# A hybrid-branch layer on one core: order of the Fourier weight products, pooling products one block earlier, the output gate multiplied into the output weights

## The chip, the cores and the metric

The program runs on one core of a Trainium2 chip. Its engines have separate instruction streams: PE (TensorE, matrix products into PSUM accumulators), DVE (VectorE) and ACT (ScalarE) for elementwise work, POOL (GpSimd), and SP (SyncE), which here only issues DMA transfers. The metric is the device time of one execution in microseconds (us), lower is better; times are medians of several runs.

## The reference, cut to what matters

One layer over 1024 latent tokens and 256 context tokens of width 1024, in float32:

```python
h = rms_norm(x + sincos) * (1 + scale) + shift            # modulated by c @ ada_w
u_lru, z_lru, u_fft, z_fft, u_pool, z_pool, gates = split(h @ w_in)
y_lru  = scan(forward) + scan(backward)                   # per-channel linear recurrences
y_fft  = einsum(real(fft2(u_fft by groups)), fft_w)       # 4 groups of 128 channels
y_pool = einsum(windowed means - u_pool, pool_w) * pool_scale   # 4 groups of 128 channels
m = sum over the branches of sigmoid(gate_b) * ((y_b * silu(z_b)) @ proj_b)
x = x + gt[None, :] * (m @ w_out)                         # gt: 1024 values, from c @ ada_w
out = rms_norm(x, final_g)
```

## The kernel before, in words

**Products.** Every large float32 product runs on TensorE as three products of a high and a low part (`mm3`, L190: low weights times high data, high times low, high times high). So each operand is first cut in two by `split` (L125): ACT copies the high part (L129), DVE subtracts to get the low part (L134). Data lies with channels on partitions, in tiles of 128 x 1024 tokens; an accumulator is one of four PSUM tiles of 128 x 1024 (`acc`), which comes free when its last reader is done.

**Middle part.** TensorE's instructions stand in the program in the order of a list of units (L1111 to L1120), worked off by one loop. A unit `("g4", 0)` is the first half of the 48 products of one 128-column block of the input projection; `m0` to `m3` are the pooling branch's products (6 each, `MP`, L1002), `c0` to `c7` that branch's output projection (24 products each, over all four pooling groups), `s`, `t` and `b` the same for the Fourier branch, `pa` for the recurrent branch. Loads and vector steps are hooked to places of this list by `on(place, function)`. Order on the other engines, SP's DMA queue among them, is set by a scheduler that simulates the program; what it chose is fixed when the kernel is built. Blocks that are not needed at once are parked in DRAM (`keep`, L84) and loaded again (`fetch`, L106).

`group_dft` (L910) computes two plain (not split) products with a 512-wide operand into the two halves of one accumulator `pq`, and splits each. `load_pool(n)` (L992) fetches one pooling tile `pp` and splits it into `ph` and `pl`; it is hooked three units ahead of `m`n, and `load_z("p", n)` two ahead. `MP` multiplies its result with `zp` on DVE and splits it again into `c`n`h` and `c`n`l`.

**Last part.** The output weights `wo` come in eight tiles; `split_wo` (L1069) splits each raw tile. `gate_rows` spreads the gate `gt` over the partitions (`gt["b"]`, a 128 x 1024 tile, called `gtb` at the end). In the last stage all engines follow the written order: for each of eight row tiles of 128 tokens there are 48 products with `wo`, then `finish` (L1236) multiplies the sums with `gtb`, adds the residual, squares with a running sum on ACT, takes the root and its reciprocal, and scales with the final gain `fgt`. The last row tile (`finish_last`, L1257) is cut in columns 0 to 511, 512 to 767 and 768 to 1023 (`CUTS`, L1255) so that its vector work follows its products closely; its first cut is multiplied with `fgt` on POOL and scaled on ACT.

Of the kernel before, what the change touches and what calls it, by code (L numbers as in the profile page):

```python
# [9 lines left out]
AF = mybir.ActivationFunctionType  # L10
ALU = mybir.AluOpType

D = 1024
# [3 lines left out]
HALF = 512  # L17
EPS = 1e-6
# [10 lines left out]
def tile_hybrid_mixer(  # L29
# [26 lines left out]
    V, S, G, PE, SP = nc.vector, nc.scalar, nc.gpsimd, nc.tensor, nc.sync  # L56
# [11 lines left out]
    def f4(name, shape=(128, 1024), pool=None):  # L68
        return (pool or p4).tile(list(shape), F32, tag="t4", name=name)

    def f2(name, shape=(128, 512)):
        return p2.tile(list(shape), F32, tag="t2", name=name)
# [4 lines left out]
    def r2(name, shape=(128, 512)):  # L77
        return p2.tile(list(shape), F32R, tag="t2", name=name)

    def acc(name):  # L80
        return pacc.tile([128, 1024], F32, tag="acc", name=name)
# [31 lines left out]
    def act(o, i, func=AF.Identity, **kw):  # L113
        S.activation(out=o, in_=i, func=func, **kw)  # L114

    def tt(o, a, b, op):
        V.tensor_tensor(o, a, b, op=op)  # L117

    def stt(o, a, s, b, op0, op1, **kw):
        V.scalar_tensor_tensor(o, a, s, b, op0=op0, op1=op1, **kw)  # L120
# [6 lines left out]
    def split(hi, lo, src, eng="act", low="dve"):  # L127
        if eng == "act":
            S.copy(hi, src)  # L129
        elif eng == "pool":  # L130
            G.tensor_scalar(hi, src, 1.0, 0.0, op0=ALU.mult, op1=ALU.add)
        else:
            V.tensor_copy(hi, src)
        (G if low == "pool" else V).tensor_tensor(lo, src, f(hi), op=ALU.subtract)  # L134
# [55 lines left out]
    def mm3(o, pairs, first=True, last=True):  # L190
        n = len(pairs)
        for i, (wh, wl, xh, xl) in enumerate(pairs):
            PE.matmul(out=o, lhsT=wl, rhs=xh, start=first and i == 0, stop=False)  # L193
            PE.matmul(out=o, lhsT=wh, rhs=xl, start=False, stop=False)  # L194
            PE.matmul(out=o, lhsT=wh, rhs=xh, start=False, stop=last and i == n - 1)  # L195
# [6 lines left out]
    eps = const.tile([128, 1], F32, name="eps")  # L202
    sc = const.tile([128, 160], F32, name="sc")
    b1 = sc[:, 0:8]
# [5 lines left out]
    c4 = sc[:, 64:80]  # L210
# [31 lines left out]
    with tc.manual_schedule(engines={ET.PE}):  # L242
# [132 lines left out]
        t0, t1, t2, t3 = tmp  # L375
# [534 lines left out]
        def group_dft():  # L910
            cg, fw = pq["cg"], pq["fw"]
            pq["h"], pq["l"] = [], []
            ps = acc("pq")
            for n in range(2):
                PE.matmul(out=ps[:, H[n]], lhsT=cg[:, n * 128:(n + 1) * 128], rhs=fw, start=True, stop=True)
                hi, lo = r2(f"pqh{n}"), r2(f"pql{n}")
                split(hi, lo, ps[:, H[n]])
                pq["h"].append(hi)
                pq["l"].append(lo)
# [144 lines left out]
        wof = {}  # L1064
# [2 lines left out]
            wof[k] = Weight(f"wo{k}", wo[k], (128, 1024), (praw,) + ((pwt, pwt) if k < 3 else (p4, p4)))  # L1067

        def split_wo(k):  # L1069
            w = wof.pop(k).ready()  # L1070
            woh[k], wol[k] = w.hi, w.lo

        diag, gt = {}, {}
# [33 lines left out]
        def halves(*keys):  # L1107
            return [(k, h) for k in keys for h in range(2)]
# [4 lines left out]
        units = halves("ZP0", "ZP1", "ZP2", "ZP3")  # L1113
        LRU_AT = {}
        for j in range(NK):
            LRU_AT[j] = len(units)
            units += halves(f"u{j}", *others[4 * j:4 * j + 4])
        units += halves("g4", "g5") + ["m0"] + halves("g6") + ["m1", "m2"] + halves("g7")
        units += ("m3 c0 c1 s0 c2 s1 t0 c3 s2 t1 c4 s3 t2 c5 t3 c6 c7 b0 b1 b2 b3 b4 b5 b6 b7").split()
        units += halves(*[f"pa{n}" for n in range(NK)])  # L1120
        pos_of = {u: n for n, u in enumerate(units)}
        wkeys = []
# [12 lines left out]
        def on(u, func, *a, table=ev):  # L1135
            u = pos_of[u] if not isinstance(u, int) else u
            table.setdefault(u, []).append(lambda: func(*a))
# [15 lines left out]
            for k, n in AT:  # L1153
                on(LRU_AT[j] + n, pieces[k], table=ev if k == "w" else aft)

        on(pos_of["g4", 0] - 1, load_poolw)
        on(pos_of["g4", 0], load_dft)
        on(pos_of["g5", 0], group_dft)
        for n in range(4):
            on(pos_of[f"m{n}"] - 3, load_pool, n)  # L1160
# [17 lines left out]
        for k in range(3):  # L1178
            on(A0 + 10 + k, load_wo, k)
            on(A0 + 12 + k, split_wo, k)  # L1180
# [15 lines left out]
        late = 0  # L1196
        flush_stores(len(units))
        assert not ev and not aft, (ev.keys(), aft.keys())
        gtb = gt.pop("b")
        for k in range(NK):  # L1200
            yh[k] = yl[k] = None

# [1 line left out]
        for k in range(3, NK):  # L1204
            load_wo(k)
            split_wo(k)
        strict.enter_context(tc.manual_schedule(engines=REST))
        fgt = f4("fgt")
# [27 lines left out]
        def finish(i):  # L1236
            o = po.pop(i)
            r = xp.pop(i)
            q = f4(f"q{i}")
            ss = rss[:, 2 * (i % 8):2 * (i % 8) + 2]  # L1240
            for h in range(2):
                sl = slice(h * HALF, (h + 1) * HALF)
                tt(q[:, sl], o[:, sl], gtb[:, sl], ALU.mult)
                tt(r[:, sl], r[:, sl], q[:, sl], ALU.add)
                act(q[:, sl], r[:, sl], AF.Square, accum_out=ss[:, h:h + 1])
            tt(ss[:, 0:1], ss[:, 0:1], ss[:, 1:2], ALU.add)
            act(ss[:, 0:1], ss[:, 0:1], AF.Sqrt, scale=1.0 / D, bias=eps)
            V.reciprocal(ss[:, 0:1], ss[:, 0:1])
            for h in range(2):
                sl = slice(h * HALF, (h + 1) * HALF)  # L1250
                stt(q[:, sl], r[:, sl], ss[:, 0:1], fgt[:, sl], ALU.mult, ALU.mult)
                SP.dma_start(out=out[i * 128:(i + 1) * 128, sl], in_=q[:, sl])


        CUTS = ((0, 512), (512, 768), (768, 1024))  # L1255

        def finish_last(i):  # L1257
            r = xp.pop(i)
            ss = rss[:, 0:4]
            parts = []  # L1260
            for n, (lo, hi) in enumerate(CUTS):
                o = acc(f"o{i}_{n}")
                mm3(o[:, 0:hi - lo], [(mh[k][:, i * 128:(i + 1) * 128], ml[k][:, i * 128:(i + 1) * 128],
                                       woh[k][:, lo:hi], wol[k][:, lo:hi]) for k in range(NK)])
                if n == 0:
                    finish(i - 1)
                p, q = f2(f"rp{n}"), f4(f"rq{n}", (128, 512))
                p, q = p[:, 0:hi - lo], q[:, 0:hi - lo]
                parts.append((p, q))
                tt(q, o[:, 0:hi - lo], gtb[:, lo:hi], ALU.mult)  # L1270
                tt(p, r[:, lo:hi], q, ALU.add)
                act(q, p, AF.Square, accum_out=ss[:, n:n + 1])
            tt(ss[:, 0:1], ss[:, 0:1], ss[:, 1:2], ALU.add)
            tt(ss[:, 0:1], ss[:, 0:1], ss[:, 2:3], ALU.add)
            act(ss[:, 0:1], ss[:, 0:1], AF.Sqrt, scale=1.0 / D, bias=eps)
            G.tensor_tensor(parts[0][0], parts[0][0], fgt[:, 0:HALF], op=ALU.mult)
            V.reciprocal(ss[:, 0:1], ss[:, 0:1])  # L1277
            for (lo, hi), (p, q) in zip(CUTS, parts):
                if lo:
                    stt(q, p, ss[:, 0:1], fgt[:, lo:hi], ALU.mult, ALU.mult)  # L1280
                else:
                    act(q, p, scale=ss[:, 0:1])
                SP.dma_start(out=out[i * 128:(i + 1) * 128, lo:hi], in_=q)


        for k in range(NK):
# [2 lines left out]
        for i in range(7):  # L1289
            if 2 < i + 3 < 8:  # L1290
                load_res(i + 3)
            if 2 < i < 6:
                WO(i + 1, range(NK), True, True)
            finish(i) if i < 6 else None
        finish_last(7)
        strict.close()

# [91 lines left out]
```

## Time and profile before

| what | value |
|---|---|
| runs | 1024.05, 1025.68, 1026.28 us; median 1025.68 |
| profiled execution | 1026.29 us, of which 1024.3 us are the span of the trace |
| TensorE busy | 993.5 us (97%) |
| VectorE busy | 604.0 us (59%) |
| ScalarE busy | 537.7 us (52%) |
| GpSimd busy | 25.1 us (2%) |
| moved by DMA | 152.59 MB, 149 GB/s on average |

The span runs from the first to the last event of the trace; the profiled execution's own time has some 2 us around it. Busy shares are means over all stages; what one stage costs is read from the rows of its own stretch. Matrix products overlap: a row's duration is longer than the step to the next row.

### The profile page before, as it was taken

Reading aid. Unit: us, or ns where it says so; the run is one execution under the profiler, and the core shown is the slowest. Engines: PE = TensorE matmul, PEld = TensorE weight load, DVE = VectorE, ACT = ScalarE, POOL = GpSimd, SP = SyncE. Lnnn points to the kernel's source line nnn. Section 1 sums busy time; section 2 is a strip of 40 time slices with the busy share of each in tenths; the row PEclk is TensorE's granted clock in tenths of the full one; section 3 lists DMA queues with packets and bytes.
Section 4 is the critical chain, followed back from the end, with each engine's and each line's share of the span. In section 5 each row is a group of like instructions: output and inputs, shape, how many; then the busy total and the mean of one; then the engine's idle time right before and its main releaser. Section 6 shows DMA issues by size and latency. Waiting matters only on the chain. (4 is left out here: it accounts for less than half of the span.)

```text
span 1024.3 us, 11615 instructions
## 1 busy us (share of the span) xinstructions
PE 993.5 (97%) x4572; PEld 821.0 (80%) x4572; DVE 604.0 (59%) x770; ACT 537.7 (52%) x632; POOL 25.1 (2%) x23
## 2 busy tenths in 40 slices
PE   7999999999999999999999999979899999999995
PEld 5867888888888888888888888858698888888885
DVE  6969286448485575936638274345465763444177
ACT  4543553793957859688694966914232221222122
POOL 0000000000000000000000000000000000000232
PEclk9999999999999999999999999989899999999998
DMA  9541694133322323343423322437445793325053
GB/s 347 196 154 42 208 411 167 66 103 132 104 83 72 124 93 124 123 154 103 154 103 116 105 78 72 148 135 272 139 170 208 265 325 129 124 103 165 19 198 121
DMA packets 47656, 152.59 MB, mean 149 GB/s; under 512 B 5489, under 2 KB 8177, under 8 KB 47602
## 3 DMA queue, kind: packets, MB, share of 16 engines
q1 hardware_dynamic: 47602, 151.85, 41.7%
q8 instruction: 36, 0.59, 0.2%
q14 instruction: 18, 0.15, 0.0%
HBM read 114.08 MB, written 37.75 MB: 148 GB/s over the span
## 5 line engine op out<-in xcount | busy, mean ns | idle before, releaser
L114 ACT ACT_TABLE_LOAD x71 | 91.1, 1283 | 1.9 <-PEq L1379 0.7
L120 DVE SCALAR_TENSOR_TENSOR junk<-ada,sb 128x1024 bf16<-128x1024 f32 x32 | 39.0, 1219 | 23.6 <-DMA ada<-in_ada 22.9
L193 PE MATMUL pg<-hh,g_l 128*128 128x512 f32 x128 | 51.3, 401 | 0.0
L194 PE MATMUL o<-wo_l,mh 128*128 128x512 f32 (+1 forms) x136 | 51.2, 377 | 0.0
L195 PE MATMUL o<-wo_h,mh 128*128 128x512 f32 (+1 forms) x136 | 51.2, 376 | 0.0
L193 PE MATMUL o<-wo_h,ml 128*128 128x512 f32 (+1 forms) x136 | 51.2, 376 | 0.0
L194 PE MATMUL pg<-hl,g_h 128*128 128x512 f32 x128 | 50.5, 395 | 0.0
L195 PE MATMUL pg<-hh,g_h 128*128 128x512 f32 x128 | 50.5, 394 | 0.0
L193 PE MATMUL ppa<-yh,pa_l 128*128 128x512 f32 x128 | 50.2, 392 | 0.0
L193 PE MATMUL ph<-hh,h_l 128*128 128x512 f32 x128 | 49.9, 389 | 0.0
L195 PE MATMUL ppa<-yh,pa_h 128*128 128x512 f32 x128 | 49.8, 389 | 0.0
L195 PE MATMUL ph<-hh,h_h 128*128 128x512 f32 x128 | 49.8, 389 | 0.0
L194 PE MATMUL ph<-hl,h_h 128*128 128x512 f32 x128 | 49.8, 389 | 0.0
L194 PE MATMUL ppa<-yl,pa_h 128*128 128x512 f32 x128 | 49.8, 389 | 0.0
L193 PE MATMUL pu<-hh,u_l 128*128 128x512 f32 x128 | 49.8, 389 | 0.0
L194 PE MATMUL pu<-hl,u_h 128*128 128x512 f32 x128 | 49.8, 389 | 0.0
L195 PE MATMUL pu<-hh,u_h 128*128 128x512 f32 x128 | 49.8, 389 | 0.0
L193 PE MATMUL pi<-hh,i_l 128*128 128x512 f32 x128 | 49.8, 389 | 0.0
L194 PE MATMUL pi<-hl,i_h 128*128 128x512 f32 x128 | 49.8, 389 | 0.0
L195 PE MATMUL pi<-hh,i_h 128*128 128x512 f32 x128 | 49.8, 389 | 0.0
L114 ACT ACTIVATE gc<-bdc,sml 64x256 f32<-64x256 f32 x64 | 30.1, 470 | 33.1 <-PE bdc L694 32.2
L117 DVE TENSOR_TENSOR i<-i,xc 128x1024 f32<-128x1024 f32 x16 | 18.9, 1224 | 44.7 <-ACT i L114 44.7
(386 smaller groups left out, 2665.8 us busy)
## 6 DMA issues: line engine op xcount, KB each, us to landing
ada<-in_ada SPq DMA_DIRECT2D x32, 512.0 KB, 9.1
x<-in_xT SPq DMA_DIRECT2D x8, 512.0 KB, 10.4
u_f<-in_w_in SPq DMA_DIRECT2D x8, 512.0 KB, 3.6
i_f<-in_w_in SPq DMA_DIRECT2D x8, 512.0 KB, 4.5
z<-k_z SPq DMA_DIRECT2D x8, 512.0 KB, 5.0
k_i<-ei SPq DMA_DIRECT2D x8, 512.0 KB, 2.8
k_y<-z SPq DMA_DIRECT2D x8, 512.0 KB, 2.6
h_f<-in_w_in SPq DMA_DIRECT2D x8, 512.0 KB, 4.6
```

What stands on the lines that cost most here:

```text
L114: S.activation(out=o, in_=i, func=func, **kw)
L117: V.tensor_tensor(o, a, b, op=op)
L120: V.scalar_tensor_tensor(o, a, s, b, op0=op0, op1=op1, **kw)
L193: PE.matmul(out=o, lhsT=wl, rhs=xh, start=first and i == 0, stop=False)
L194: PE.matmul(out=o, lhsT=wh, rhs=xl, start=False, stop=False)
L195: PE.matmul(out=o, lhsT=wh, rhs=xh, start=False, stop=last and i == n - 1)
```

## The change

Four things change. In `group_dft` both products are issued before either split. The list of units has `m0` to `m3` one block of the input projection earlier, and their loads with them; the pooling weights are loaded one more unit ahead. `split_wo` multiplies each raw tile of output weights by the gate, and the products with `gtb` in `finish` and `finish_last` are gone. In `finish_last` the first two cuts are multiplied with `fgt` on DVE as they come, GpSimd's product is gone, the sum of squares of two cuts and the root's argument are prepared ahead of the third, and the three stores go out in another order, one of them issued by ACT.

```diff
@@ -913,6 +913,7 @@
             ps = acc("pq")
             for n in range(2):
                 PE.matmul(out=ps[:, H[n]], lhsT=cg[:, n * 128:(n + 1) * 128], rhs=fw, start=True, stop=True)
+            for n in range(2):
                 hi, lo = r2(f"pqh{n}"), r2(f"pql{n}")
                 split(hi, lo, ps[:, H[n]])
                 pq["h"].append(hi)
@@ -1067,7 +1068,9 @@
             wof[k] = Weight(f"wo{k}", wo[k], (128, 1024), (praw,) + ((pwt, pwt) if k < 3 else (p4, p4)))
 
         def split_wo(k):
-            w = wof.pop(k).ready()
+            w = wof.pop(k)
+            tt(w.raw, w.raw, gt["b"], ALU.mult)
+            w.ready()
             woh[k], wol[k] = w.hi, w.lo
 
         diag, gt = {}, {}
@@ -1115,8 +1118,8 @@
         for j in range(NK):
             LRU_AT[j] = len(units)
             units += halves(f"u{j}", *others[4 * j:4 * j + 4])
-        units += halves("g4", "g5") + ["m0"] + halves("g6") + ["m1", "m2"] + halves("g7")
-        units += ("m3 c0 c1 s0 c2 s1 t0 c3 s2 t1 c4 s3 t2 c5 t3 c6 c7 b0 b1 b2 b3 b4 b5 b6 b7").split()
+        units += halves("g4") + ["m0"] + halves("g5") + ["m1", "m2"] + halves("g6") + ["m3"] + halves("g7")
+        units += ("c0 c1 s0 c2 s1 t0 c3 s2 t1 c4 s3 t2 c5 t3 c6 c7 b0 b1 b2 b3 b4 b5 b6 b7").split()
         units += halves(*[f"pa{n}" for n in range(NK)])
         pos_of = {u: n for n, u in enumerate(units)}
         wkeys = []
@@ -1153,7 +1156,7 @@
             for k, n in AT:
                 on(LRU_AT[j] + n, pieces[k], table=ev if k == "w" else aft)
 
-        on(pos_of["g4", 0] - 1, load_poolw)
+        on(pos_of["g4", 0] - 2, load_poolw)
         on(pos_of["g4", 0], load_dft)
         on(pos_of["g5", 0], group_dft)
         for n in range(4):
@@ -1196,7 +1199,6 @@
         late = 0
         flush_stores(len(units))
         assert not ev and not aft, (ev.keys(), aft.keys())
-        gtb = gt.pop("b")
         for k in range(NK):
             yh[k] = yl[k] = None
 
@@ -1240,8 +1242,7 @@
             ss = rss[:, 2 * (i % 8):2 * (i % 8) + 2]
             for h in range(2):
                 sl = slice(h * HALF, (h + 1) * HALF)
-                tt(q[:, sl], o[:, sl], gtb[:, sl], ALU.mult)
-                tt(r[:, sl], r[:, sl], q[:, sl], ALU.add)
+                tt(r[:, sl], o[:, sl], r[:, sl], ALU.add)
                 act(q[:, sl], r[:, sl], AF.Square, accum_out=ss[:, h:h + 1])
             tt(ss[:, 0:1], ss[:, 0:1], ss[:, 1:2], ALU.add)
             act(ss[:, 0:1], ss[:, 0:1], AF.Sqrt, scale=1.0 / D, bias=eps)
@@ -1267,20 +1268,24 @@
                 p, q = f2(f"rp{n}"), f4(f"rq{n}", (128, 512))
                 p, q = p[:, 0:hi - lo], q[:, 0:hi - lo]
                 parts.append((p, q))
-                tt(q, o[:, 0:hi - lo], gtb[:, lo:hi], ALU.mult)
-                tt(p, r[:, lo:hi], q, ALU.add)
+                tt(p, o[:, 0:hi - lo], r[:, lo:hi], ALU.add)
                 act(q, p, AF.Square, accum_out=ss[:, n:n + 1])
-            tt(ss[:, 0:1], ss[:, 0:1], ss[:, 1:2], ALU.add)
-            tt(ss[:, 0:1], ss[:, 0:1], ss[:, 2:3], ALU.add)
-            act(ss[:, 0:1], ss[:, 0:1], AF.Sqrt, scale=1.0 / D, bias=eps)
-            G.tensor_tensor(parts[0][0], parts[0][0], fgt[:, 0:HALF], op=ALU.mult)
-            V.reciprocal(ss[:, 0:1], ss[:, 0:1])
-            for (lo, hi), (p, q) in zip(CUTS, parts):
-                if lo:
-                    stt(q, p, ss[:, 0:1], fgt[:, lo:hi], ALU.mult, ALU.mult)
+                if n < 2:
+                    tt(p, p, fgt[:, lo:hi], ALU.mult)
+                if n == 1:
+                    tt(ss[:, 0:1], ss[:, 0:1], ss[:, 1:2], ALU.add)
+                    V.tensor_scalar(ss[:, 0:1], ss[:, 0:1], 1.0 / D, EPS, op0=ALU.mult, op1=ALU.add)
+            act(ss[:, 2:3], ss[:, 2:3], AF.Sqrt, scale=1.0 / D, bias=ss[:, 0:1])
+            V.reciprocal(ss[:, 2:3], ss[:, 2:3])
+            for n in (2, 0, 1):
+                (lo, hi), (p, q) = CUTS[n], parts[n]
+                if n == 2:
+                    stt(q, p, ss[:, 2:3], fgt[:, lo:hi], ALU.mult, ALU.mult)
+                elif n:
+                    V.tensor_scalar(q, p, ss[:, 2:3], 0.0, op0=ALU.mult, op1=ALU.add)
                 else:
-                    act(q, p, scale=ss[:, 0:1])
-                SP.dma_start(out=out[i * 128:(i + 1) * 128, lo:hi], in_=q)
+                    act(q, p, scale=ss[:, 2:3])
+                (SP if n else S).dma_start(out=out[i * 128:(i + 1) * 128, lo:hi], in_=q)
 
 
         for k in range(NK):
```

On SP's queue, in the stretch around the weight products of `group_dft`, the order before was as follows (`k_` marks a store into a parking place; `pp` are pooling tiles, `zp` their factors, `k_y7` the last result of the recurrent branch, `pc` projection weights):

```order
L99 DMA k_y7_4817<-z7_4777 128x1024
L107 DMA zp0_4900<-k_ZP0_1007 128x1024
L99 DMA k_g4_4887<-eg4_4885 128x1024
L140 DMA pc2_f_5197<-in_pc 128x1024
L107 DMA pp1_4961<-k_UP1_1992 128x1024
L99 DMA k_g5_4959<-eg5_4957 128x1024
L140 DMA pc3_f_5306<-in_pc 128x1024
L107 DMA zp1_4979<-k_ZP1_1106 128x1024
L107 DMA pp2_4981<-k_UP2_2443 128x1024
```

and it is now:

```order
L107 DMA zp0_4830<-k_ZP0_1007 128x1024
L99 DMA k_g3_4817<-eg3_4815 128x1024
L140 DMA pc1_f_5125<-in_pc 128x1024
L99 DMA k_y7_4823<-z7_4783 128x1024
L107 DMA pp1_4891<-k_UP1_1992 128x1024
L99 DMA k_g4_4889<-eg4_4887 128x1024
L140 DMA pc2_f_5197<-in_pc 128x1024
L107 DMA zp1_4920<-k_ZP1_1106 128x1024
L107 DMA pp2_4922<-k_UP2_2443 128x1024
```

`zp0` now stands ahead of `k_y7`. `pp1` is the first issue behind that store (the fourth before), and `pp2` the fifth; before, `pp2` stood behind `k_g5` too, the result of the next block.

On DVE, the last row tile before (`o` are its accumulators, `rp` and `rq` its work tiles, `xr` the residual, `sc` the small sums):

```order
L117 TENSOR_TENSOR xr6_6954<-xr6_6954,q6_7182 128x512
L117 TENSOR_TENSOR q6_7182<-o6_7094,gtb_6173 128x512
L117 TENSOR_TENSOR xr6_6954<-xr6_6954,q6_7182 128x512
L117 TENSOR_TENSOR sc_83<-sc_83 128x1
L1248 RECIPROCAL sc_83<-sc_83 128x1
L120 SCALAR_TENSOR_TENSOR q6_7182<-xr6_6954,sc_83,fgt_6670 128x512 x2
L117 TENSOR_TENSOR rq0_7197<-o7_0_7157,gtb_6173 128x512
L117 TENSOR_TENSOR rp0_7196<-xr7_7024,rq0_7197 128x512
L117 TENSOR_TENSOR rq1_7227<-o7_1_7201,gtb_6173 128x256
L117 TENSOR_TENSOR rp1_7226<-xr7_7024,rq1_7227 128x256
```

and now:

```order
L1249 RECIPROCAL sc_83<-sc_83 128x1
L120 SCALAR_TENSOR_TENSOR q5_7141<-xr5_6937,sc_83,fgt_6678 128x512 x2
L117 TENSOR_TENSOR xr6_6956<-o6_7092,xr6_6956 128x512 x2
L117 TENSOR_TENSOR sc_83<-sc_83 128x1
L1249 RECIPROCAL sc_83<-sc_83 128x1
L120 SCALAR_TENSOR_TENSOR q6_7178<-xr6_6956,sc_83,fgt_6678 128x512 x2
L117 TENSOR_TENSOR rp0_7190<-o7_0_7153,xr7_7024 128x512
L117 TENSOR_TENSOR rp0_7190<-rp0_7190,fgt_6678 128x512
L117 TENSOR_TENSOR rp1_7220<-o7_1_7195,xr7_7024 128x256
L117 TENSOR_TENSOR rp1_7220<-rp1_7220,fgt_6678 128x256
```

The three products with `gtb` are gone, two products with `fgt` stand ahead of the third cut, and one sum of `sc` and the argument of the root are worked out before the third cut's sum.

## Rows read from the trace of the kernel before

**Rows 1.** The page, part 1: busy time, share of the span, instructions by engine.

```profile
PE 993.5 (97%) x4572; PEld 821.0 (80%) x4572; DVE 604.0 (59%) x770; ACT 537.7 (52%) x632; POOL 25.1 (2%) x23
```

**Rows 2.** Who TensorE waited for: engine, line, releaser: us in total, times, longest.

```profile
PE pq L915 <- DVE pql L134: 5.8, 1, 5.8
...
PE p L193 <- ACT c3h L129: 3.8, 1, 3.8
PE z L360 <- ACT wz_h L129: 2.5, 1, 2.5
PE psb L505 <- DVE vz L117: 1.4, 1, 1.4
```

**Rows 3.** Order in time, TensorE, weight products: start us, us, engine, line, operation.

```profile
668.93 1.02 PE L915 MATMUL pq<-fw,cg 128*128 128x512 f32 x2
...
681.50 0.39 PE L193 MATMUL pg<-hh,g_l 128*128 128x512 f32 x1
```

**Rows 4.** Granted clock by stretch: us, engines' busy us, PEclk, DMA share, GB/s.

```profile
64.00:66.00 2.00, 2.00 (x5) 1.61 (x6) 2.00 (x2) 0.30 (x1) 0.00 (x0) 0.50 0.00 0
99.00:102.00 3.00, 2.75 (x12) 1.01 (x13) 3.00 (x6) 1.87 (x2) 0.00 (x0) 1.00 0.00 0
677.00:679.00 2.00, 2.00 (x6) 1.19 (x5) 0.48 (x1) 0.59 (x1) 0.00 (x0) 0.50 0.89 266
```

**Rows 5.** Order in time, TensorE, two plain products like those of rows 3.

```profile
847.88 1.88 PE L1087 MATMUL gt<-dg,ones 128*128 128x512 f32 x4
...
849.83 0.40 PE L194 MATMUL ppa<-yl,pa_h 128*128 128x512 f32 x1
```

**Rows 6.** Order in time, TensorE, first products of the pooling branch's projection.

```profile
719.36 0.39 PE L195 MATMUL p<-c2h,pc_h 128*128 128x512 f32 x1
...
729.28 0.40 PE L195 MATMUL p<-c2h,pc_h 128*128 128x512 f32 x1
```

**Rows 7.** Order in time, TensorE, one weight block between two pooling products.

```profile
691.71 0.39 PE L193 MATMUL pg<-hh,g_l 128*128 128x512 f32 x1
...
702.59 0.39 PE L193 MATMUL mp<-ph,pwl 128*128 128x512 f32 x1
```

**Rows 8.** Order in time, the DMA issue queue of SyncE.

```profile
674.02 0.32 SPq L99 DMA_DIRECT2D k_y<-z  x1
...
675.75 0.43 SPq L140 DMA_DIRECT2D pc_f<-in_pc  x1
676.27 1.28 SPq L107 DMA_DIRECT2D pp<-k_UP  x1
```

**Rows 9.** DMA issues from 674 to 677 us: count, size, us to landing.

```profile
pc_f<-in_pc SPq DMA_DIRECT2D x1, 512.0 KB, 7.8
pp<-k_UP SPq DMA_DIRECT2D x1, 512.0 KB, 8.6
```

**Rows 10.** Order in time, ScalarE, the cast of a pooling tile.

```profile
700.13 1.05 ACT L129 CAST ph<-pp 128x1024 fp32r<-128x1024 f32 x1 [5.44 <-DMA pp<-k_UP]
```

**Rows 11.** Order in time, VectorE, output projections.

```profile
893.37 1.22 DVE L117 TENSOR_TENSOR gt<-gt,ppa 128x1024 f32<-128x1024 f32 x1 [5.05 <-PE ppa L195]
```

**Rows 12.** Order in time, TensorE, last product of the program.

```profile
1013.04 0.28 PE L195 MATMUL o<-wo_h,mh 128*128 128x256 f32 x1
```

**Rows 13.** Order in time, VectorE, the last two row tiles.

```profile
1009.03 0.68 DVE L117 TENSOR_TENSOR q<-o,gtb 128x512 f32<-128x512 f32 x1
...
1016.12 0.42 DVE L117 TENSOR_TENSOR rq<-o,gtb 128x256 f32<-128x256 f32 x1
...
1019.21 0.16 DVE L117 TENSOR_TENSOR sc<-sc 128x1 f32<-128x1 f32 x1 [0.51 <-ACT rq L114]
...
1019.93 0.88 DVE L120 SCALAR_TENSOR_TENSOR rq<-rp,sc,fgt 128x256 f32<-128x256 f32 x2
```

**Rows 14.** Order in time, ScalarE, the last square.

```profile
1018.67 0.42 ACT L114 ACTIVATE rq<-rp 128x256 f32<-128x256 f32 x1 [1.02 <-DVE rp L117]
```

**Rows 15.** Order in time, SyncE's last issues.

```profile
1020.74 1.30 SPq L1283 DMA_DIRECT2D out<-rq  x3
```

## The prediction

> **What bounds the kernel now.** I read the page's busy shares first, then the list of what TensorE waited for, then the order in time around each of those waits with the granted clock beside it, and last the end of the span. TensorE is busy 97% of the span [rows 1], so a microsecond is gained where TensorE waits, where its clock is low, or after its last product. VectorE at 59% and ScalarE at 52% (the table above) set nothing on average, only at single places.
>
> The list of waits names them [rows 2]: 5.8 us before the second plain product `pq` of `group_dft`, 3.8 us in the first `c` unit for `c3h`, 2.5 us and 1.4 us at places that the change leaves alone. A long wait costs more than itself. In the stretch after the 2.5 us wait and in that after the 5.8 us wait the granted clock is 0.50, which is 1.2 GHz; after the 1.4 us wait it is 1.00, 2.4 GHz [rows 4]. So I take a wait of 2.5 us or more to bring a stretch at 1.2 GHz, and one of 1.4 us not to.
>
> At the end, TensorE starts its last product at 1013.04 [rows 12], VectorE ends its last scaling at 1019.93 + 0.88 = 1020.81 [rows 13], and SyncE issues the three last stores from 1020.74 [rows 15]. Between product and scaling VectorE is late: it begins the seventh row tile at 1009.03 [rows 13], though the eighth tile's products alone take as long as a weight block, 702.59 − 691.71 = 10.88 us [rows 7], so that the seventh tile's sums were there at 1013.2 − 10.88 = 1002.3. VectorE is 6.7 us behind.
>
> **Term 1, both `pq` products before either split.** Before, the second product stood behind the first split. It wrote into the accumulator that this split was reading, and the split's subtraction was queued on VectorE behind other work. Now nothing stands between the two. At 2.4 GHz two plain products (two records each) and one step of an ordinary product took 847.88 to 849.83, 1.95 us [rows 5]; less that step of 0.227 us (10.88 / 48) this is 1.72 us for the two. From 668.93 the tenth product of the next block then starts at 668.93 + 1.72 + 9 × 0.227 = 672.69; it started at 681.50 [rows 3]. Gain 8.8 us: the wait of 5.8 us, and 3 us of half clock. What is late next is the accumulator's release, after both subtractions. It is needed by the block after next, 10.88 us later, and two subtractions of 0.68 us (a 128 x 512 operation of rows 13) fit there with several microseconds to spare.
>
> **Term 2, `m3` one block earlier.** Before, `c0` came right after `m3`, and `c0` needs all four pooling tiles. Twelve steps at full clock after 719.36 would be 722.08; the product that stands there started at 729.28 [rows 6]. Now `g7`'s 10.88 us [rows 7] stand between `m3` and `c0`. What has to happen in them is one product with `zp`, one copy and one subtraction, of 1.22 us, 1.05 us and 1.22 us by operations of this size [rows 10, 11]: 3.5 us. Gain 7.2 us; spare 7 us.
>
> **Term 3, the loads that have to come earlier.** This is the cost. TensorE reaches `m2` at 668.93 + 1.72 + 10.88 (`g5`) + 2 × 1.36 (`m0` and `m1`, six products each of 0.227 us) = 684.25. Its tile `pp2` comes from SyncE's queue, and there it and `pp1` stand behind the store `k_y7`, the order above shows. That store waits for the recurrent branch's last product on VectorE and was issued at 674.02 [rows 8]. I keep that time, since the work ahead of it on VectorE and ScalarE is nearly the same; one more copy of 1.05 us could come ahead of it. `pp2` is the sixth issue of the cluster that `k_y7` opens. Before, the fourth, `pc_f` at 675.75, took 7.8 us to land and the fifth, `pp` at 676.27, took 8.6 [rows 8, 9]: landings at 683.6 and 684.9, a step of 1.3 us. The sixth then lands at 686.2, and with the copy of 1.05 us [rows 10] `ph2` is there at 687.25. TensorE waits 3.0 us, and a little more for the low part. The wait of 3.8 us in term 2 cost 7.2 us in all; one shorter by 0.8 us costs 6.4 us. `pp1`, second of the cluster, would land by the same steps near 681.0 and be copied by 682.1, in time for `m1` at 682.9.
> Bounds: nothing, if the cluster starts 3 us sooner or lands as one tile alone would; 3.5 us, if it waits but the clock stays up; 8.8 us, if `k_y7` is another 1.05 us late and `m1` waits too, so that its six products run at half clock (1.36 us more). I take 6.4, the size of the nearest wait (`c3h`).
>
> [...]
>
> **Term 4, the gate in the output weights.** Each of eight raw weight tiles gets one product of 128 x 1024, 1.22 us of VectorE [rows 11]: 9.8 us in all, during the projection of the recurrent branch and at the start of the last stage. VectorE has 5.05 us of idle time per block of 10.88 us there [rows 11], so a block carries its one to two extra products and the splits stay ahead of the products that need them; I cost it at nothing. Without that cover it is 1.22 us for each tile that comes late.
> In the last stage each of the tiles loses two products of 0.68 us [rows 13]. Over the six tiles before the seventh this is 8.2 us, more than the 6.7 that VectorE was behind. So it is on time when the last cut's sums come.
>
> **Term 5, the tail.** After the last product, from 1013.04 to 1013.3 [rows 12], comes one addition of 0.42 us [rows 13] to 1013.7. From the last square to the end of the scaling took 1018.67 to 1020.81, 2.14 us [rows 13, 14]. The sum that started at 1019.21, 0.16 us long [rows 13], is out of that chain now, so the scaling ends at 1015.7 instead of 1020.81: 5.1 us. The products with `fgt` in VectorE's rows stand ahead of the third cut's sum, in the 2.7 us that TensorE needs for that cut's 24 products of half width (24 × 0.227 / 2). GpSimd's product, which was to overlap the end, is gone. Three store issues took 1.30 us [rows 15]; with one of them on ScalarE's queue SyncE's last one goes out 0.43 us earlier. Together 5.5 us. No row shows a store issued by ScalarE. Nearest rows: it costs what an issue of SyncE's costs, and saves 0.4 us; or the scaling and issue on ScalarE end last, up to 1.3 us later (all three issues in a row). I take the saving, since ScalarE has nothing else to do there.
>
> The Trainium skill ("DMA: Bandwidth & Descriptors", "Issuing engines are not separate DMA queues") says that transfers started by different engines run on the same DMA engines, and that only the issuing time is saved. By that the store's change of queue can't give more than the 0.4 us; with no saving at all the sum would be 0.4 us higher.
>
> **Sum.** −8.8 − 7.2 + 6.4 + 0 − 5.5 = −15.1 us. The profiled execution took 1026.29 us (span 1024.3), so 1011.2. It lay 0.6 us over the median of the runs, 1025.68; on that scale 1010.6.
>
> **The rivals.**
> *B, no new wait at `m2`, or one without the slow clock.* For it: the landings of rows 9 were measured in a cluster that also carried a `zp` load and a store early in it, and the order ahead of `pp1` is shorter now. Against it: 3 us are missing, twice an issue step. Without a wait −21.5 us gives 1004.2; with 3.5 us of wait and a full clock 1007.7.
> *C, the tail gives about 1 us.* VectorE could still be behind, if the last stage is paced by something other than VectorE's count (ScalarE's roots, GpSimd's additions to the residual), or the store from ScalarE ends last. Then the last tile alone loses 0.68 + 2 × 0.42 = 1.5 us of products with `gtb`, gains 0.68 + 0.42 = 1.1 us of products with `fgt`, and one sum and one issue go (0.16 + 0.43): 1.0 us. For it: the backlog is worked out, not read from one row. Against it: 8.2 us are taken off 6.7. Time 1010.6 + 4.5 = 1015.1.
> *D, the change does not do what it says: the second `pq` product still waits*, because its accumulator was held by something other than the split. Against it: the list of waits names `pql` as the releaser [rows 2]. TensorE would then reach `m2` 8.8 us later and not wait there; what is left is 7.2 + 5.5, 1013.0.
> *E, slower: `k_y7` late.* `pp1` and `pp2` can't be issued before `k_y7`, and that one waits for the recurrent branch. Every microsecond that the branch's last product slips is one at `m1` and `m2`, where before `pp2` had a block of 10.88 us to spare. The copies and subtractions for `m0` now stand among that branch's steps on ScalarE and VectorE. The gain is eaten when the product ends 15 us later, at 689 instead of 674; at 18 us the time is 1028.6. For it: the place of `k_y7` in the order above. Against it: the work that comes between is one copy and one subtraction, some 2.3 us [rows 10, 11].
>
> **Chances and range.** Forecast 0.55 (own range 1007.5 to 1013.5, from a cost of 3.5 to 8.8 us in term 3), B 0.22, C 0.11, D 0.05, E 0.07. Of E 0.04 is slower and 0.02 no change; slips of a microsecond or two lie in the forecast's own range. About 0.2% is what a measurement of this kernel can tell from no change. So faster 0.94, same 0.02, slower 0.04. The range takes in B without a wait, and C: 1003.5 to 1016.
>
> **What would show it.** In the profile after: no wait at `pq`, and the two `pq` products in 1.72 us (term 1); no wait for `c3h` (term 2); a wait of about 3 us at `mp` for the copy of a late `pp`, and a granted clock of 0.50 behind it (term 3); no wait for a low part of `wo` (term 4); VectorE's seventh tile begun near 1002 on the old scale, and 2.7 us from TensorE's last start to the end of the last scaling instead of 7.8 (term 5). The prediction is wrong if TensorE waits somewhere else for 3 us or more, if `mp` does not wait, or if the tail stays over 5 us.

## The result: 17 us faster, where 15 were predicted

The changed kernel takes 1008.44 us (median of 4 runs, 1007.72 to 1009.21), the kernel before 1025.72 us (4 runs). The ratio is 0.9834, 95% interval 0.9821 to 0.9846. Predicted were 1010.6 us, with a range from 1003.5 to 1016. The profiled execution of the changed kernel took 1009.21 us with a span of 1007.1 us.

**The profile after.** Who TensorE waited for, as in [rows 2]:

```profile
PE psb L505 <- DVE vz L117: 2.5, 1, 2.5
PE z L360 <- ACT wz_h L129: 2.5, 1, 2.5
...
PE mp L193 <- ACT ph L129: 0.8, 1, 0.8
PE mp L194 <- DVE pl L134: 0.8, 1, 0.8
PE p L193 <- DVE al L134: 0.5, 1, 0.5
```

The waits for `pql` (5.8 us) and for `c3h` (3.8 us) are gone. Two new ones stand at `mp`, 0.8 us each, which are the high and the low part of `pp2`. A small one of 0.5 us for `al`, in the projection that follows, is not in the list before; it is no effect of the change, since e3 and e4, whose middle part is the old one, have it with 0.9 and 0.3 us, and r3, the changed kernel once more, has none. The wait for `psb`, which no edit touches, is 2.5 us instead of 1.4.

TensorE in the order of time at the places of [rows 3] and at `m0` and `m2` (start us, us, engine, line, operation):

```profile
670.19 0.39 PE L193 MATMUL mp<-ph,pwl 128*128 128x512 f32 x1
...
671.55 1.88 PE L915 MATMUL pq<-fw,cg 128*128 128x512 f32 x4
672.87 0.79 PE L193 MATMUL pg<-hh,g_l 128*128 128x512 f32 x1
...
675.36 0.39 PE L193 MATMUL pg<-hh,g_l 128*128 128x512 f32 x1
...
685.33 0.39 PE L195 MATMUL mp<-ph,pwh 128*128 128x512 f32 x1
686.52 0.51 PE L193 MATMUL mp<-ph,pwl 128*128 128x512 f32 x1 [0.80 <-ACT ph L129]
687.78 0.51 PE L194 MATMUL mp<-pl,pwh 128*128 128x512 f32 x1 [0.76 <-DVE pl L134]
...
689.05 0.39 PE L193 MATMUL pg<-hh,g_l 128*128 128x512 f32 x1
```

Both `pq` products are now one row, with no wait in it. The tenth product of the block after them starts at 675.36, which is 3.81 us after 671.55; worked out were 1.72 + 9 × 0.227 = 3.76. `m1` is left at 685.33 + 0.23 = 685.56, and the next block starts at 689.05; `m2`'s six products need 1.36 us of these 3.49, so 2.13 us are lost.

The granted clock by stretch, of the changed kernel, as in [rows 4]:

```profile
64.00:66.00 2.00, 1.94 (x8) 1.27 (x9) 2.00 (x2) 0.36 (x1) 0.00 (x0) 1.00 0.00 0
101.00:103.00 2.00, 2.00 (x6) 0.61 (x5) 2.00 (x5) 1.29 (x2) 0.00 (x0) 0.50 0.00 0
686.00:688.00 2.00, 0.73 (x2) 0.41 (x3) 1.50 (x2) 2.00 (x3) 0.00 (x0) 1.00 0.01 2
688.00:690.00 2.00, 2.00 (x10) 1.62 (x10) 2.00 (x3) 0.34 (x1) 0.00 (x0) 1.00 0.43 168
```

Around `m2` the clock stays at 1.00. At the start of the program the two places have changed roles: behind the 2.5 us wait for `wz_h` the clock is 1.00 now (0.50 before), and behind `psb` it is 0.50 (1.00 before). The two go together in all 13 profiled executions of this document: where the clock behind `wz_h` was low, the wait for `psb` is 1.2 to 1.5 us, where it was full, 2.5 to 2.6.

The tail, answering to [rows 12 to 15], first TensorE's last product, then VectorE, then ScalarE with the store that it issues (ACTq), then SyncE:

```profile
1001.16 0.28 PE L195 MATMUL o<-wo_h,mh 128*128 128x256 f32 x1
```

```profile
997.31 0.69 DVE L117 TENSOR_TENSOR rp<-rp,fgt 128x512 f32<-128x512 f32 x1 [0.84 <-ACT rq L114]
...
999.72 0.43 DVE L117 TENSOR_TENSOR rp<-rp,fgt 128x256 f32<-128x256 f32 x1 [0.64 <-ACT rq L114]
...
1001.48 0.42 DVE L117 TENSOR_TENSOR rp<-o,xr 128x256 f32<-128x256 f32 x1 [1.07 <-PE o L195]
...
1003.40 0.35 DVE L1285 TENSOR_SCALAR rq<-rp,sc 128x256 f32<-128x256 f32 x1
```

```profile
1003.00 0.72 ACT L114 ACTIVATE rq<-rp,sc 128x512 f32<-128x512 f32 x1 [0.23 <-DVE sc L1279]
1003.75 0.37 ACTq L1288 DMA_DIRECT2D out<-rq  x1
```

```profile
1003.51 0.81 SPq L1288 DMA_DIRECT2D out<-rq  x2
```

VectorE now waits for TensorE (1.07 us before the last cut), where it was behind before. From TensorE's last start to the end of the last scaling are 1003.40 + 0.35 − 1001.16 = 2.6 us, before 7.8. ScalarE's scaling ends at 1003.72, and its store goes out while SyncE issues the other two.

**Where the time went**, by three marks that both traces have:

| stretch | before | after | difference |
|---|---|---|---|
| start to the end of block `g4` | 668.93 | 670.19 | +1.3 |
| from there to TensorE's last start | 344.11 | 330.97 | −13.1 |
| from there to the end of the span | 11.26 | 5.94 | −5.3 |
| span | 1024.3 | 1007.1 | −17.2 |

The first row is the start of the program, which the change doesn't touch; what it is comes below. The last row rests on one profile before, and the old tail is not always as long: e1 and e2 below, which leave it alone, have 10.67 and 9.78 us there.

### The profile page after: what moved, and what is told of

It reads as the page before. It is cut to its first block, busy times and chain, and to the rows that moved or that the text cites. A ratio compares the mean times of both kernels' runs of the same rounds, so it can differ in the third digit from the quotient of the medians.

```text
span 1007.1 us, 11592 instructions
## 1 busy us (share of the span) xinstructions
PE 988.1 (98%) x4572; PEld 816.9 (81%) x4572; DVE 598.6 (59%) x763; ACT 537.3 (53%) x632; POOL 21.6 (2%) x22
## 4 chain that ended last, share of the span: by engine, by line
PE 82%; ACT 3%; DVE 2%; DMA 1%; issue 1%; SPq 0%; DVEq 0%; ACTq 0%
PE o L195 3%; PE o L194 3%; PE o L193 3%; PE ppa L195 3%; PE ph L194 3%; PE ppa L193 3%; PE ph L195 3%; PE pu L194 3%; PE pi L195 3%; PE ph L193 3%; PE pu L195 3%; PE pu L193 3%; PE pi L194 3%; PE pi L193 3%; PE ppa L194 3%; PE p L193 3%
```

## The experiments

The terms were separated by doing each part of the change alone on the kernel before (e1 to e4), then the one cost that had been mis-sized was moved in both directions (e5 to e7), then the store was undone (e8), and two kernels were run again (r1 to r3).

**e1: both `pq` products first, alone.**

```diff
             for n in range(2):
                 PE.matmul(out=ps[:, H[n]], lhsT=cg[:, n * 128:(n + 1) * 128], rhs=fw, start=True, stop=True)
+            for n in range(2):
                 hi, lo = r2(f"pqh{n}"), r2(f"pql{n}")
```

> The kernel before with one part of the change, both pq products ahead of both splits; the units, the gate and the tail are the old ones. My theory (the terms add, each at its own place): the 5.8 us wait and the half clock behind it go, 8.8 us, so 1016.9 us; the 3.8 us wait for c3h stays with its half clock, since m3 and c0 still stand side by side. Rival (the gain is given back further on): TensorE reaches m1, m2 and c0 8.8 us earlier, the loads behind SyncE's queue don't, and a new wait or a longer one for c3h takes half or more: 1021 us or above.

Measured: 1017.06 us against 1025.94, ratio 0.9914 (0.9899 to 0.9928), 8.9 us less. The wait for `c3h` in its trace:

```profile
PE p L193 <- ACT c3h L129: 3.7, 1, 3.7
```

The gain is whole, 8.9 where 8.8 were expected, and the wait for `c3h` is as long as before. Nothing is given back further on: the rival falls.

**e2: the list of units, alone.**

```diff
-        units += halves("g4", "g5") + ["m0"] + halves("g6") + ["m1", "m2"] + halves("g7")
-        units += ("m3 c0 c1 ...
+        units += halves("g4") + ["m0"] + halves("g5") + ["m1", "m2"] + halves("g6") + ["m3"] + halves("g7")
+        units += ("c0 c1 ...
...
-        on(pos_of["g4", 0] - 1, load_poolw)
+        on(pos_of["g4", 0] - 2, load_poolw)
```

> The kernel before with the new list of units and the pooling weights loaded one unit earlier; group_dft, gate and tail as before. My theory: the c3h wait of 3.8 us goes with its half clock, 7.2 us; the pq wait stays, and since it holds TensorE back by 8.8 us, the tiles for m1 and m2 are there and neither waits: 1018.5 us. Rival (the new wait for a pooling tile belongs to the order of units itself): m2 waits here too, some 2 us as in the changed kernel, 1020.6 us, or more with a low clock.

Measured: 1017.56 us, ratio 0.9920 (0.9907 to 0.9934), 8.2 us less by the ratio. Neither `c3h` nor `mp` is in its list of waits. The first `pq` product and the second, in time:

```profile
669.59 1.02 PE L915 MATMUL pq<-fw,cg 128*128 128x512 f32 x2
676.00 2.07 PE L915 MATMUL pq<-fw,cg 128*128 128x512 f32 x2 [5.39 <-DVE pql L134]
```

The second product comes hardly later than in [rows 3] and its row (675.79), though `m0`'s six products now stand ahead of it: the wait for `pql` is 5.4 us instead of 5.8, and `m0` runs in part inside time that was lost before. In the changed kernel this is not to be had, since `pq` doesn't wait there. It is small: from the end of `g4` (668.23) the second product comes 7.77 us later, before 6.86, so 0.9 of the 1.36 us of `m0` are still paid. The measured 8.2 us have an interval of 6.8 to 9.5 and are not clear of the 7.2 expected. In the trace the middle, between the marks of the table above, is 6.8 us shorter, with a wait of 0.9 us for `al` in it; the rest of its gain stands at the start (0.7 us) and in the tail (1.5 us), which no edit touches.

**e3: the gate in the output weights, alone, with the old tail.** `split_wo` and `finish` as in the change, and in `finish_last` only

```diff
-                tt(q, o[:, 0:hi - lo], gtb[:, lo:hi], ALU.mult)
-                tt(p, r[:, lo:hi], q, ALU.add)
+                tt(p, o[:, 0:hi - lo], r[:, lo:hi], ALU.add)
```

> The kernel before with the gate multiplied into the output weights and the products with gtb gone from all row tiles; group_dft, units and the order of the last tile's tail (GpSimd's product, sums at the end, three stores on SyncE) as before. My theory: the end was late because VectorE was 6.7 us behind; without the 12 products it is on time, and the old tail order then costs hardly more than the new one: 4.9 us gained, 1020.8 us. Rival (the gain of the end comes from the new order of the last tile): 1 to 2 us gained, about 1024 us. A wait for a low part of wo would show that the products in split_wo are not hidden.

Measured: 1021.62 us, ratio 0.9955 (0.9942 to 0.9968), 4.6 us less by the ratio. VectorE and TensorE at the end:

```profile
1002.81 1.29 DVE L117 TENSOR_TENSOR xr<-o,xr 128x512 f32<-128x512 f32 x2 [6.65 <-issue]
...
1013.94 0.42 DVE L117 TENSOR_TENSOR rp<-o,xr 128x256 f32<-128x256 f32 x1 [2.39 <-PE o L195]
...
1015.66 0.88 DVE L120 SCALAR_TENSOR_TENSOR rq<-rp,sc,fgt 128x256 f32<-128x256 f32 x2
```

```profile
1013.63 0.28 PE L195 MATMUL o<-wo_h,mh 128*128 128x256 f32 x1
```

VectorE is on time for the seventh tile (1002.81 against 1009.03 in [rows 13]) and waits 2.39 us for the last product. From TensorE's last start to the end of the scaling are 2.9 us with the old order of the tail, 2.6 with the new one in the changed kernel. The list of waits has none for a part of `wo`: the eight products in `split_wo` are hidden.

**e4: the new order of the last tile, alone, with `gtb` kept.** `finish_last` as in the change, but

```diff
-                tt(p, o[:, 0:hi - lo], r[:, lo:hi], ALU.add)
+                tt(q, o[:, 0:hi - lo], gtb[:, lo:hi], ALU.mult)
+                tt(p, r[:, lo:hi], q, ALU.add)
```

> The kernel before with the new order of the last tile alone (products with fgt on VectorE, sums early, root with the first sum as its bias, stores 2, 0, 1 with one of them from ScalarE); the products with gtb stay in all tiles. My theory: VectorE is still 6.7 us behind when it comes to the last tile, the two fgt products add 1.1 us to its queue and the sum, one issue and the collision with GpSimd's product take 1.4 away: about 0.3 us gained, 1025.4 us. Rival: the new order is what made the end short, 4 to 5 us gained, 1021 us.

Measured: 1027.16 us (12 runs), ratio 1.0012 (1.0003 to 1.0020): 1.2 us slower, where 0.3 us faster was expected. Both theories miss; mine has the wrong sign. VectorE's rows of the last tile:

```profile
1015.07 0.68 DVE L117 TENSOR_TENSOR rq<-o,gtb 128x512 f32<-128x512 f32 x1
...
1017.37 0.69 DVE L117 TENSOR_TENSOR rp<-rp,fgt 128x512 f32<-128x512 f32 x1 [0.84 <-ACT rq L114]
...
1019.54 0.43 DVE L117 TENSOR_TENSOR rp<-rp,fgt 128x256 f32<-128x256 f32 x1 [0.62 <-ACT rq L114]
```

The two products with `fgt` overwrite the tile that ScalarE is squaring, so each waits for the square: 0.84 and 0.62 us, beside 0.69 and 0.43 us of their own. While VectorE is behind, these 2.6 us are on the path. Against them stand 0.8 us, since the last addition no longer runs beside GpSimd's product (0.42 us); in the trace before it took 1.22:

```profile
1017.42 1.22 DVE L117 TENSOR_TENSOR rp<-xr,rq 128x256 f32<-128x256 f32 x1
```

So the last tile takes VectorE 7.8 us from 1015.07 to the end of the last scaling; in the traces before, of e1 and of e2 it is 6.1. The time from TensorE's last start to the end of the span doesn't show this against the trace before (11.44 us for 11.26), because VectorE came to this tile only 0.2 us after TensorE's last start there and 1.7 us in the trace before: how far it is behind differs between executions. e2, with the old order, came to it 0.2 us after as well, and has 9.78. The rest by which this profiled execution is longer, the slowest of the twelve, lies ahead of the tail.

In the changed kernel the same waits are in VectorE's rows (0.84 and 0.64 us at 997.31 and 999.72), but there it has to wait for TensorE anyway. So the new order costs a microsecond as long as the backlog is there, and gives 0.3 to 0.5 us once it is gone, by the traces of e3 and of the changed kernel.

**e5: the changed kernel, pooling tiles loaded two units earlier.**

```diff
-            on(pos_of[f"m{n}"] - 3, load_pool, n)
+            on(pos_of[f"m{n}"] - 5, load_pool, n)
```

> The changed kernel with load_pool hooked five units ahead of its product instead of three, so that pp1 and pp2 stand on SyncE's queue ahead of k_y7. My theory: both tiles are there when m1 and m2 come, the wait at m2 (two parts of 0.8 us in the changed kernel, 2.1 us of time with its slower first products) goes, and nothing else: 1006.3 us. Rival (another wait takes its place): the earlier loads hold buffers or delay what the recurrent branch still needs, z7 ends later, and the time is 1008 us or more.

Measured: 1006.12 us, ratio 0.9815 (0.9801 to 0.9829) to the kernel before; e8, which ran beside it and differs from the changed kernel only in a store, took 1008.52. SyncE's queue and `m2`, in time:

```profile
668.12 0.38 SPq L107 DMA_DIRECT2D pp<-k_UP  x1
675.72 0.32 SPq L99 DMA_DIRECT2D k_y<-z  x1
```

```profile
684.87 0.39 PE L195 MATMUL mp<-ph,pwh 128*128 128x512 f32 x1
685.10 0.39 PE L193 MATMUL mp<-ph,pwl 128*128 128x512 f32 x1
```

`pp2` (668.12) is issued 7.6 us ahead of `k_y7` (675.72), and `m2`'s products follow `m1`'s without a gap. `k_y7` does come late here, 6.0 us after the end of `g4` where the changed kernel has 4.8, as the rival held, but no wait follows from it. This is the fastest version that ran: it beats both kernels.

**e6: the changed kernel, `pp2` one issue later.**

```diff
-            on(pos_of[f"m{n}"] - 3, load_pool, n)
+            on(pos_of[f"m{n}"] - (3, 3, 1, 3)[n], load_pool, n)
```

> The changed kernel with the load of pp2 hooked two units later, which puts it one issue further back on SyncE's queue, behind zp2. My theory: the tile lands 0.6 to 1.3 us later and m2 waits so much longer, at a full clock: 1009.4 us. Rival (the clock falls as soon as the wait nears 2 us, as the prediction took it): 3 us more, about 1012.4 us, with a granted clock of 0.50 behind the wait.

Measured: 1010.89 us (1009.09 to 1012.18), ratio 0.9860 (0.9846 to 0.9874), between the two expectations and with a spread of its own. In the profiled execution the wait is 2.1 + 0.8 us and the clock does fall:

```profile
PE mp L193 <- ACT ph L129: 2.1, 1, 2.1
...
PE mp L194 <- DVE pl L134: 0.8, 1, 0.8
```

```profile
689.00:690.00 1.00, 1.00 (x4) 0.81 (x3) 0.40 (x1) 0.00 (x0) 0.00 (x0) 0.50 1.02 377
```

So the rival is right for that execution, but not in its price: from `m2`'s first product to `m3`'s are 15.04 us here and 13.41 in the changed kernel (686.52 to 699.93), so the low clock cost 1.6 us, not 3. Whether the length of the wait decides was the question for r1 and r2.

**r1, r2: the same kernel, two more executions.**

> The changed kernel with pp2 loaded one issue later, once more, as it is. My theory: the wait at m2 is the same as in the earlier execution of this kernel (2.1 us and 0.8 us), but the clock behind it is not bound to it: 0.50 again costs 1010.8 us, 1.00 some 3 us less in that stretch, with the start of the program (0 or 1.3 us) on top. Rival (the length of the wait decides): a granted clock of 0.50 behind it in every execution.

> The same kernel a third time, with the same two expectations: either clock (mine), or 0.50 each time (rival).

Measured: 1009.95 and 1010.59 us, one execution each. The same stretch with the first products of `m2` and `m3`, first in r1, then in r2:

```profile
689.00:690.00 1.00, 1.00 (x4) 0.72 (x4) 0.80 (x1) 0.00 (x0) 0.00 (x0) 0.50 1.01 385
```

```profile
685.57 0.50 PE L193 MATMUL mp<-ph,pwl 128*128 128x512 f32 x1 [1.76 <-ACT ph L129]
...
700.58 0.39 PE L193 MATMUL mp<-ph,pwl 128*128 128x512 f32 x1
```

```profile
689.00:690.00 1.00, 1.00 (x5) 0.83 (x6) 1.00 (x1) 0.00 (x0) 0.00 (x0) 1.00 0.99 340
```

```profile
687.67 0.50 PE L193 MATMUL mp<-ph,pwl 128*128 128x512 f32 x1 [2.00 <-ACT ph L129]
...
701.06 0.39 PE L193 MATMUL mp<-ph,pwl 128*128 128x512 f32 x1
```

r1 waited 1.8 + 0.8 us and ran on at 0.50; r2 waited 2.0 + 0.8 us, a little longer, and ran on at 1.00. The length of the wait doesn't decide by itself. From `m2` to `m3` r1 takes 15.01 us and r2 13.39, so the low clock cost 1.6 us, half of the 3 expected. The whole times hide even that: r1 is the shorter one, since `g4` ended at 668.29 in it and at 670.14 in r2, which ran the products behind `psb` at 0.50.

**r3: the changed kernel, one more execution.**

> The changed kernel once more. My theory: at m2 two waits of 0.8 us and a granted clock of 1.00 as in its first profile, 2.1 us lost; at the start either clock behind the 2.5 us wait for wz_h. Rival: the half clock behind m2 comes here too in some executions, and the loss is then near 5 us.

Measured: 1007.91 us. Waits of 0.9 and 0.8 us at `m2`, and a clock of 1.00 behind them again. e8, which has the same loads, is a third such execution (0.6 and 0.8 us, clock 1.00). Three executions do not exclude a low one.

**e7: the changed kernel, `pp2` behind `k_g5`.** The same edit with `(3, 3, 0, 3)`.

> The changed kernel with the load of pp2 hooked three units later, behind the store k_g5 on SyncE's queue, which comes only after g5's products. My theory: pp2 is issued near 687.5, lands near 693.5 and is copied by 694.5 on the changed kernel's scale, m2 waits some 9 us, and a wait of that length does bring a stretch at half clock: 7.6 us of wait and 3 us of clock more, about 1019 us. Rival (what a wait costs is only its length; the half clock in the kernel before had another reason): 1016 us, clock 1.00 behind the wait.

Measured: 1016.72 us, ratio 0.9918 (0.9904 to 0.9932), 8.3 us above the changed kernel. In the time of its trace:

```profile
684.76 0.39 PE L195 MATMUL mp<-ph,pwh 128*128 128x512 f32 x1
693.07 0.79 PE L193 MATMUL mp<-ph,pwl 128*128 128x512 f32 x1 [7.92 <-ACT ph L129]
...
696.62 0.60 PE L193 MATMUL pg<-hh,g_l 128*128 128x512 f32 x1
697.05 0.41 PE L194 MATMUL pg<-hl,g_h 128*128 128x512 f32 x1
```

```profile
694.00:696.00 2.00, 1.68 (x4) 1.39 (x5) 1.50 (x2) 0.33 (x1) 0.00 (x0) 0.50 1.02 410
```

The wait is 7.9 us, 7.1 more than the changed kernel's, and the clock behind it is 0.50, as I held. But from `m2`'s first product to the next block it is 3.55 us where the changed kernel needs 689.05 − 686.52 = 2.53, and one step of that block is 0.2 longer: the stretch is 1.2 us longer, although its wait for `pl` is 0.3 us shorter (0.47 and 0.76). So the half clock cost 1.5 us, where I had put 3. It had fallen at 690.2 already, while TensorE was still waiting, and was back by 697.1, so only some 3.5 us of work ran at it; in the trace before, the low clock around `pq` lasts from 674.7 to 681.5, and TensorE was at work in all of it from 675.79 on. That brings e7 to the rival's number without the rival's reason.

**e8: all three last stores on SyncE.**

```diff
-                (SP if n else S).dma_start(out=out[i * 128:(i + 1) * 128, lo:hi], in_=q)
+                SP.dma_start(out=out[i * 128:(i + 1) * 128, lo:hi], in_=q)
```

> The changed kernel with all three last stores issued by SyncE. My theory: the third issue of SyncE comes 0.4 us later and with it the end: 1008.8 us. Rival (the store from ScalarE ends last or starts slower than one from SyncE): the same time or up to 1 us less, 1007.5 to 1008.4 us.

Measured: 1008.52 us, ratio 0.9839 (0.9825 to 0.9853); the changed kernel 0.9834. The expected 0.4 us is less than these runs can tell. In the traces 6.09 us lie between TensorE's last start and the end of the span in e8 and 5.94 in the changed kernel, 0.15 us; the seven profiled executions with the store on ScalarE's queue have 5.91 to 5.99. So the saving is nearer 0.1 than 0.4 us by the traces, and the times can't tell it from nothing. The bound of 1.3 us more for that store is excluded by the traces.

## Why the prediction was right, step by step

**Terms 1 and 2: shown.** The `pq` products and the tenth product after them take on the new trace what was worked out, and e1 measured 8.9 us for 8.8. The wait for `c3h` is gone in the changed kernel and in e2, and e2's 8.2 us agree with 7.2 within its interval.

**Term 3 was mis-sized: 2.1 us in the profile instead of 6.4.** The step was named rightly (`pp2` on SyncE's queue behind `k_y7`, a wait at `m2` for the copy), and e5 shows that taking it away gives 2 us. Two numbers in it were wrong.
The first is the landing. Worked out was `ph2` at 687.25, which on the later start of the new trace (+1.26) is 688.5; it was there at 685.42 + 1.05 = 686.47, 2.0 us earlier. 0.3 us of that is `k_y7` (675.01 instead of 675.28). The rest is how [rows 9] was read: I took the landings of 683.6 and 684.9 as the pace of a busy queue. The stretches of the kernel before show something else:

```profile
682.00:683.00 1.00, 1.00 (x6) 0.84 (x5) 0.00 (x0) 0.00 (x0) 0.00 (x0) 1.00 0.44 176
683.00:684.00 1.00, 1.00 (x6) 0.81 (x5) 0.00 (x0) 0.00 (x0) 0.00 (x0) 1.00 0.07 29
684.00:685.00 1.00, 1.00 (x6) 0.84 (x5) 0.00 (x0) 0.00 (x0) 0.00 (x0) 1.00 0.02 8
```

The last two numbers are the mean busy share of the DMA engines and GB/s. At 683 the transfers are all but over: 0.07 of 16 engines is about one engine's work. The last landing came with this remainder, 2 us after the bulk; why it trails isn't shown. In the changed kernel the engines are busy to the end, and the landing comes with it:

```profile
684.00:685.00 1.00, 1.00 (x6) 0.84 (x5) 0.39 (x1) 0.00 (x0) 0.00 (x0) 1.00 1.08 442
685.00:686.00 1.00, 0.72 (x4) 0.26 (x2) 0.00 (x0) 0.58 (x1) 0.00 (x0) 1.00 0.60 246
```

```profile
685.42 1.05 ACT L129 CAST ph<-pp 128x1024 fp32r<-128x1024 f32 x1 [2.58 <-DMA pp<-k_UP]
```

The step of 1.3 us from one tile to the next was right (the last landings of the new cluster are 682.8, 684.1 and 685.4); the time from which it was counted was some 2 us late.
The second is the clock. I took 2.9 us of half clock behind the wait (6.4 less rival B's 3.5), from one profiled execution. After the wait that did come the clock stayed up, in all three executions (the two of the changed kernel, and e8). Where it fell at this place, in e6, r1 and e7, it cost 1.5 to 1.6 us. e6, r1 and r2 show both outcomes behind waits of nearly equal length, and the 2.5 us wait for `wz_h` is followed by 0.50 in the kernel before and by 1.00 in the one after. The Trainium skill ("TensorE: Matmul & The Clock Gate", "What's actually happening") says of the start of a kernel that the number of slow products differs from run to run of one kernel. r1 against r2 shows the like behind a wait in the middle. Rival B, a wait at a full clock, was the better description of this step; its price of 3.5 us was still too high.

**Term 4 and term 5: right, 5.3 us in the trace for 5.5.** That is against the longest of three old tails; against those of e1 and e2 it is 4.7 and 3.8 us. e3 and e4 divide the 5.3. Of them the 12 products taken off VectorE give 4.8 (e3's last start to end of span is 1020.1 − 1013.63 = 6.5 us, before 11.3), the new order and the store 0.5 more, and only together with the first. The prediction had both in one term, and its price for rival C (1 us gained by the tail while VectorE is behind) was too good: that sum has 1.5 us for the last tile's products with `gtb` in it, without which it is 0.5 us lost; e4, which keeps them, lost 1.2.

**Rival D** is excluded by e1, **E** by the time of `k_y7`: it came 0.3 us earlier on the common scale, not 15 us later. That a late issue at this place is paid in full is real: e7's `pp2`, one block later, costs 8 us.

**The sum.** −8.8 − 7.2 + 2.1 − 5.3 = −19.2 us of the change; +1.3 of the start and a rest of +0.7 in the middle, of which 0.5 is the wait for `al`, make the measured −17.2 of the spans. The medians differ by 17.3. The parts alone measured −8.9, −8.2 and −4.6 us, together −21.7, each give or take 1.4; with the wait at `m2` this is −19.6, which agrees with the whole within these intervals and no closer.
The start's 1.3 us is no effect of the change. The products with `psb` begin at 99.25 in the profile before and at 99.29 in the one after; the first sixteen take 3.7 us at the clock of 1.00 before and 5.3 us after, where it fell to 0.50 among them. Of the six executions that waited 2.5 or 2.6 us for `psb` the clock fell in four (the two of the changed kernel, e5 and r2) and stayed up in two (e3 and e8). The kernel of e6, r1 and r2 has a full one in r1 and a low one in r2. So it changes from execution to execution and adds to the spread of the runs.

**What was luck.** With 2.1 us in place of 6.4 in term 3, the prediction's own sum is −19.4 us, or 1006.3, which is rival B's case. The measured 1008.44 lies between this and the forecast. That the forecast came as near as 2.2 us is in part due to things that were not in it: the 1.3 us of the start and the 0.7 us of the middle made up for half of what term 3 had too much.

## What to carry to other kernels

A wait of the engine that bounds the kernel may be moved by taking away its cause, but what the earlier work then needs has to be followed through the issue queue, and its landing read against the DMA engines' activity, not from the longest row alone. Where an engine works off a backlog at the end, the work taken from every tile pays there, and a rearrangement of the last tile pays only after the backlog is gone. A stretch of low clock behind a wait is a risk with a price, not a certain cost; ask more than one execution before adding it to a sum. The same holds for a backlog at the end, and for a small gain read from one pair of traces: compare the same stretch in the traces of several runs.

## What the runs showed of the hardware

A wait of 1.8 + 0.8 us was followed by a granted clock of 0.50 (1.2 GHz) and one of 2.0 + 0.8 us by 1.00 (2.4 GHz), in two executions of one kernel. The 2.5 us wait for `wz_h`, the same in all 13 profiled executions, was followed by a low clock in seven and by a full one in six. The same wait gave both: 2.5 to 2.6 us for `psb` was followed by a low clock in four executions and by a full one in two. The low stretch cost 3.0 us behind the `pq` wait of 5.8 us (8.8 in all), but 1.5 us behind a longer one of 7.9 us (e7), where the clock fell 2.9 us before the wait ended, and 1.6 us behind the waits of about 2 + 0.8 us (e6, r1) and behind `psb` (the products there took 5.3 us for 3.7). The landing of a 512 KB load was reported 2 us after the mean share of the 16 DMA engines had fallen to 0.07. The last tile of the old order found VectorE 0.2 to 1.7 us behind TensorE's last start in four executions of the same code for the tiles before it (the kernel before, e1, e2, e4).
